# Moving the modulation products and the scores in a two-layer retention/mLSTM trunk

## The chip, the cores and the metric

The kernel runs on one core of a Trainium2 chip, as one program. The core has a matrix engine (TensorE, PE in the profile), three engines for elementwise work (VectorE or DVE, ScalarE or ACT, GpSimd or POOL) and SyncE (SP), which here only issues transfers from the chip's main memory. Each engine runs its own list of instructions in order; the engines wait for each other through semaphores, and a transfer is waited for in the same way. The metric is the device time of one execution in microseconds (us), as the median of several.

## The reference

The reference computes two decoder layers on 512 tokens of width 1024, in float32. In layer 0 the token mixer is retention with four heads, in layer 1 it is an mLSTM with four heads; each is followed by a gated convolutional feed-forward part. Before each of these four parts the state is normed and modulated by six vectors that come from the condition `c`:

```python
c_act = jax.nn.silu(c)
for i in range(DEPTH):
    mod = c_act @ ada_w[i] + ada_b[i]
    sh_t, sc_t, gt_t, sh_f, sc_f, gt_f = [m[:, None, :] for m in jnp.split(mod, 6, axis=-1)]
    h = rmsnorm(x, norm_tok_g[i]) * (1.0 + sc_t) + sh_t
    y = retention_mixer(h, ...) if i % N_MIXERS == 0 else mlstm_mixer(h, ...)
    x = x + gt_t * y
    h = rmsnorm(x, norm_ffn_g[i]) * (1.0 + sc_f) + sh_f
    x = x + gt_f * conv_ffn(h, ...)
return rmsnorm(x, final_g)
```

The product `c_act @ ada_w[i] + ada_b[i]` gives 6 x 1024 numbers for each layer. A head of a mixer needs its projections q, k, v and g (the gate); then scores between keys and queries with a decay (retention) or with exponential gates (mLSTM); the scores times v; a group norm over the head; the gate; and the product with `w_out`, which is added to the state.

## The kernel before, in words

**Layout and precision.** The state `x` and all activations lie transposed: 128 features on the partitions, the 512 tokens along the free dimension. Every float32 operand of a matrix product is kept as a high and a low half, so that one product is three matmuls (L281 to L283, `mm3`: high times high, low times high, high times low). An activation is split into `Pair`s (`split`: the high part on ScalarE, the low part on VectorE, L277 and L278). A weight tile is loaded into `raw` by SyncE (L182), its high part `whi` is made on ScalarE (L164) and its low part `wlo` on VectorE (L169).

**Items.** The program is first collected as a list of items (`item`). Most items are one weight tile's products: a tile of q, k or g (`proj_item`, 8 x 3 matmuls of 512 columns), a quarter of a head's v (`v_items`, which fills four PSUM banks and splits them after its fourth item, `vl`), or a tile of `w_out` with the residual add. Others have no weight and call a step of a head. At the end of the program the items are run through in order; `Ahead` issues the loads and the splits of coming weight tiles some items early. On each engine the framework's scheduler then sets the order of the instructions, from its own estimates, when the program is built; inside the folded part (below) the order is the written one. So the order on an engine need not be that of the list.

**Heads.** `heads` is used by both layers. It sets the order of the four heads' steps: q(i) (four items), v(i), the scores S(i), g(i), the attention A_(i), `mid_` (centring for the group norm), `end_` (the norm's root and the gate product y) and the output tiles o(i). For a head i of 1 or 2 the scores stand right behind v(i) and ahead of g(i). The scores (`ml_scores` in layer 1) load a row `mb` and a row `db` through SyncE, broadcast over the partitions, make the weights `w` from them, multiply the products `psc` by them (`sp`) and split the result (`sh`, `sl`) in four strips of 512, 384, 256 and 128 columns. In layer 0 the weights are a decay tile, `tab`. The attention (`pav`) takes these strips times v, and is followed in layer 1 by the denominator (`pden`). `mid_` sums the head (`zs`, whose low part is `zsl`; product `pmu`) and its squares (`zv`, added on GpSimd; low part `zvl`); `end_` multiplies these (`pvar`), takes a reciprocal root (`grs`) and makes the four tiles y.

**Modulations.** A modulation is one column of 128 of the 12,288 numbers: SyncE loads a 128 x 1025 block of `ada_w` (512.5 KB) into one of the two buffers of the pool `asides`, and VectorE multiplies it by `c_ext` and sums along the row (L140, `gemv`, through `side_work`). The first 16 are made at the start. The other 80 wait in the list `side`. The loop at the end of the program takes them off it, behind items that have weights and are `free`: ahead of the first folded part one for each such item, two for every tenth item, until LATER = 32 are left; behind it one for each item with an odd number. Eight of the 32 are taken inside the folded part of layer 0 itself (`modulate`): there the load is issued in every second unit, and the product follows `low_24` of a later unit. The scheduler is asked to keep these products in program order.

**Folded part.** Most of the feed-forward part of a layer runs in `folded`. It forms sums of weight halves first (`wa`, `wb`, `ws`, `wt`), so that fewer products are needed; the low parts of three of the sums are made by an accumulating transfer that GpSimd issues (L176). The weight chunks of the down product share the pool `asides`. In this case its units run from about 495 to 735 us in layer 0 and from about 1261 to 1506 us in layer 1. `bars` holds the item numbers of these two parts.

Of the kernel before, what the change touches and what calls it, by code (L numbers as in the profile page):

```python
# [15 lines left out]
P = 128  # L16
T = 512
D = 1024
KT = D // P
# [9 lines left out]
RAWS = 6  # L29
LATER = 32  # L30
FOLD_FROM = 5
# [4 lines left out]
SPLIT = 4  # L36
# [34 lines left out]
def trunk(ctx: ExitStack, tc: tile.TileContext, xT, cb, pos, vec, decay, zmask, ada, w_s0, w_in0, w_v0,  # L71
# [29 lines left out]
    def aside(s):  # L101
        return asides.tile([P, D + 1], F32, tag="a", name=uid(s))
# [306 lines left out]
    def folded(folds, h, terms, pairs, downs, modulate):  # L409

        no = lambda *a: None
        banks, sums, other = {}, {}, []

# [24 lines left out]
        def unit(i):  # L440
# [129 lines left out]
    def v_items(w_v, hd, h, v, split, between=lambda j: None):  # L570
# [18 lines left out]
        for j in range(4):  # L589
            item([Use(w_v[hd, j], 2 * T)], mk(j))  # L590
            between(j)
# [37 lines left out]
    def boundary(late, last, norm):  # L629


        for u, _ in late + last:
            u.off = OFF
        for p, after in ((0, lambda m: norm.square(0, m)), (1, norm.later)):
            for n, (u, run) in enumerate(late):
                item([u], lambda w, run=run, p=p, n=n: run(w[0], *HALVES[p], lead=p + n == 0), False)
                if p:
                    norm.beside()
            for u, run in last:
                item([u], lambda w, run=run, p=p, after=after: run(w[0], *HALVES[p], after), False)  # L640
        norm.rest()
# [37 lines left out]
    class Start(Norm):  # L679
# [24 lines left out]
        def rest(self):  # L704
# [4 lines left out]
            def products(w, p, k0, k1):  # L709
# [8 lines left out]
            item(uses, lambda w: products(w, 0, 0, SPLIT), False)  # L718
# [3 lines left out]
            item(uses, lambda w: products(w, 0, SPLIT, KT), False)  # L722
            item([], lambda w: self.use(1, 4, 8))
# [5 lines left out]
            if self.folded:  # L729
                item([], lambda w: self.sums())  # L730
            item(uses, end, False)

# [142 lines left out]

    def heads(st, q, v, s, g, a, mid, end, o, norm, at_last):

# [9 lines left out]
        v(1, at(1, mid_, 0))  # L887
        S(1)
        end_(0)
        g(1)  # L890
        A_(1)
# [3 lines left out]
        v(2, at(0, end_, 1))  # L895
        S(2)
        g(2)
        A_(2)
# [16 lines left out]
    class Ffn:  # L915
# [77 lines left out]
        def items(self, norm):  # L993
# [3 lines left out]
            downs = [p for gi in range(len(GROUPS) - 1) for p in self.down(gi)]  # L997
            steps, run = folded(folds, self.h, self.start.terms, pairs, downs, self.layer == 0)

# [235 lines left out]

    def ret_g(i):
        for j in range(4):
            proj_item(w_in0[i * 8 + 4 + j], h0, ret_gate(i))

    def ret_o(i):  # L1240
# [4 lines left out]
          ret_scores, ret_g, ret_attend, lambda i: None, ret_end, ret_o,  # L1245
          ffn0.start, RET_LAST)

# [118 lines left out]

    def ml_g(i):
        for j in range(4):
            proj_item(w_in1[1 + i * 8 + 4 + j], h1, ml_gate(i))

# [3 lines left out]
    def ml_v(i, between=nothing):  # L1374
# [6 lines left out]
    heads(M, ml_q, ml_v, ml_scores, ml_g, ml_attend, lambda i: gn_center(M[i]), ml_end, ml_o,  # L1381
          ffn1.start, ML_LAST)
    ffn1.items(End())
# [14 lines left out]
    for n, (uses, fn, free) in enumerate(items):  # L1398
        while ahead.at < len(ahead.flat) and ahead.may(n):
            ahead.load()  # L1400
            ahead.high()
            ahead.low()
        fn([u.chunk for u in uses])
        if not uses or not free or n <= 6:
            continue
        if n < bars[0]:
            for _ in range(2 if n > 20 and n % 10 == 0 else 1):
                if len(side) > LATER:
                    side_work(*side.pop(0))
        elif side and n % 2:  # L1410
            side_work(*side.pop(0))
    assert not side
# [104 lines left out]
```

## Time and profile before

| what | value |
|---|---|
| median of 3 runs | 1560.03 us (1559.39 to 1560.14) |
| the profiled execution | 1554.46 us |
| its span, from the first to the last instruction | 1552.7 us |
| mean granted TensorE clock | 0.992 |
| instructions | 23173 |
| VectorE, busy | 1200.5 us (77%) |
| ScalarE, busy | 861.2 us (55%) |
| GpSimd, busy | 229.3 us (15%) |

All times inside the kernel are from one profiled execution and are counted from its first instruction. A row of the profile names the source line, the engine, the operation, and output <- input by the names of the program, without buffer numbers; `wlo<-raw,whi` is the low part of a weight tile. In a timeline, a row begins with its start and its length, and what stands in brackets at its end is how long the engine was idle before it and what it waited for. SPq and POOLq are the queues on which SyncE and GpSimd issue transfers. A matmul's recorded end is modelled: successive matmuls overlap in the rows, and the distance between their starts tells their real pace. Short waits of TensorE can therefore show up as a longer distance between starts and not as idle time.

### The profile page before, as it was taken

What the parts mean: (1) busy time and instruction counts of PE and PEld (TensorE: products, weight loads), DVE (VectorE), ACT (ScalarE), POOL (GpSimd) and SP (SyncE); (2) the same over time, 40 slices, a digit from 0 to 9 for tenths busy, and PEclk for the clock granted to TensorE, in tenths of its full rate; (3) what the DMA queues carried; (4) which work ended last, traced back from release to release, by engine and by line L of the source; (5) the groups of instructions that cost most, each with busy time, mean ns of one, the idle gap of its engine ahead of it and who ended that gap; (6) DMA issues with size and microseconds to landing.
All of it is one profiled execution on the core that took longest, in us unless ns stands there. A gap on an engine that the chain in (4) does not pass through costs nothing. (4 is left out here: it accounts for less than half of the span.)

```text
span 1552.7 us, 23173 instructions
## 1 busy us (share of the span) xinstructions
PE 1513.2 (97%) x8996; PEld 1337.2 (86%) x8996; DVE 1200.5 (77%) x1814; ACT 861.2 (55%) x1282; POOL 229.3 (15%) x242
## 2 busy tenths in 40 slices
PE   7999999999999999999999999999999999999997
PEld 4788888888988999998988878888889889999997
DVE  8985768786997878887777777777588977787775
ACT  4534524443456767676655554554545666767763
POOL 3421001110130111111110011001022201111102
PEclk9999999999999999999999999999999999999999
DMA  8753464655315888887444433443312258777751
GB/s 312 228 186 109 143 188 159 204 177 167 110 42 136 210 208 205 230 195 202 160 128 149 149 109 105 152 144 112 126 54 72 67 135 198 195 191 188 187 140 55
DMA packets 72224, 241.79 MB, mean 156 GB/s; under 512 B 9761, under 2 KB 12065, under 8 KB 72114
## 3 DMA queue, kind: packets, MB, share of 16 engines
q1 hardware_dynamic: 59730, 195.22, 38.4%
q0 software_dynamic: 12384, 45.09, 15.3%
q8 instruction: 70, 1.15, 0.3%
q14 instruction: 40, 0.33, 0.1%
HBM read 193.06 MB, written 2.12 MB: 126 GB/s over the span
## 5 line engine op out<-in xcount | busy, mean ns | idle before, releaser
L164 ACT CAST whi<-raw 128x1024 fp32r<-128x1024 f32 (+1 forms) x190 | 194.3, 1029 | 144.4 <-PE pp L282 58.3
L169 DVE TENSOR_TENSOR wlo<-raw,whi 128x1024 fp32r<-128x1024 f32 (+1 forms) x158 | 191.5, 1219 | 46.7 <-ACT whi L164 46.1
L281 PE MATMUL pp<-hh,whi 128*128 128x512 f32 x560 | 218.4, 390 | 2.3 <-DVE vl L278 2.0
L282 PE MATMUL pp<-hl,whi 128*128 128x512 f32 x560 | 218.1, 390 | 0.0
L283 PE MATMUL pp<-hh,wlo 128*128 128x512 f32 x560 | 218.0, 389 | 0.0
L595 DVE SCALAR_TENSOR_TENSOR x<-po,mod,x 128x512 f32<-128x512 f32 (+1 forms) x184 | 114.2, 629 | 71.6 <-PE po L283 68.0
L282 PE MATMUL po<-ggl,whi 128*128 128x512 f32 (+1 forms) x448 | 154.0, 345 | 0.0
L283 PE MATMUL po<-ggh,wlo 128*128 128x512 f32 (+1 forms) x448 | 153.5, 344 | 0.0
L281 PE MATMUL po<-ggh,whi 128*128 128x512 f32 (+1 forms) x448 | 153.0, 345 | 0.0
L422 PE MATMUL p<-hh,whi 128*128 128x256 f32 x544 | 150.6, 277 | 0.0
L423 PE MATMUL p<-hl,whi 128*128 128x256 f32 x544 | 150.4, 276 | 0.0
L424 PE MATMUL p<-hh,wlo 128*128 128x256 f32 x544 | 150.4, 276 | 0.0
L140 DVE SCALAR_TENSOR_TENSOR ada<-ada,c_ext 128x1025 f32<-128x1025 f32 x93 | 115.7, 1245 | 32.3 <-DMA ada<-ada 32.2
L281 PEld LDWEIGHTS pp<-hh,whi 128*128 128x128 f32 x560 | 105.2, 188 | 24.6 <-DVE vl L278 2.5
L283 PEld LDWEIGHTS pp<-hh,wlo 128*128 128x128 f32 x560 | 105.2, 188 | 21.8
L282 PEld LDWEIGHTS pp<-hl,whi 128*128 128x128 f32 x560 | 105.2, 188 | 21.4
L281 PE MATMUL po<-yh,whi 128*128 128x256 f32 (+1 forms) x352 | 115.8, 329 | 0.0
L282 PE MATMUL po<-yl,whi 128*128 128x256 f32 (+1 forms) x352 | 115.6, 328 | 0.0
L283 PE MATMUL po<-yh,wlo 128*128 128x256 f32 (+1 forms) x352 | 115.6, 328 | 0.0
L927 ACT ACTIVATE cv<-p,vecs 128x512 f32<-128x512 f32 x68 | 53.1, 780 | 96.2 <-PE p L424 57.3
L932 DVE SCALAR_TENSOR_TENSOR cv<-p,vecs,cv 128x511 f32<-128x511 f32 (+1 forms) x136 | 101.0, 745 | 2.2
L422 PEld LDWEIGHTS p<-hh,whi 128*128 128x128 f32 x544 | 102.2, 188 | 0.1
(287 smaller groups left out, 3986.9 us busy)
## 6 DMA issues: line engine op xcount, KB each, us to landing
ada<-ada SPq DMA_DIRECT2D x96, 512.5 KB, 4.0
raw<-w_in SPq DMA_DIRECT2D x62, 512.0 KB, 3.8
wb<-w_up SPq DMA_DIRECT2D x34, 512.0 KB, 4.4
wa<-w_up SPq DMA_DIRECT2D x34, 512.0 KB, 5.3
wlo<-wa POOLq DMA_DIRECT2D x34, 512.0 KB, 4.6
wlo<-ws POOLq DMA_DIRECT2D x34, 512.0 KB, 4.9
raw<-w_o SPq DMA_DIRECT2D x32, 512.0 KB, 3.5
raw<-w_dn SPq DMA_DIRECT2D x32, 512.0 KB, 4.4
```

The source lines that it names most:

```text
L140: return V.scalar_tensor_tensor(raw, raw, 1.0, c_ext[:], op0=ALU.mult, op1=ALU.mult, accum_out=mods[layer][:, f : f + 1])
L164: A.copy(hi, w[:, r])
L169: V.tensor_tensor(lo, w[:, r], hi.bitcast(F32), op=ALU.subtract)
L281: PE.matmul(o, ah, bh, start=start, stop=False)
L282: PE.matmul(o, ah, bl, start=False, stop=False)
L283: PE.matmul(o, al, bh, start=False, stop=stop)
L422: PE.matmul(o, hi[:, ch], b[0], start=st, stop=False, skip_group_check=True)
L423: PE.matmul(o, hi[:, ch], b[1], start=False, stop=False, skip_group_check=True)
L424: PE.matmul(o, lo[:, cl], b[0], start=False, stop=sp, skip_group_check=True)
L595: V.scalar_tensor_tensor(x[m][:, r], ps[:, r], gate_col, x[m][:, r], op0=ALU.mult, op1=ALU.add)
L927: A.activation(acc[:], ps[:], AF.Identity, bias=col("fcb", self.layer * 2 * FT + f), scale=self.conv_col(f, 2))
L932: V.scalar_tensor_tensor(acc[:, s:], ps[:, : T - s], self.conv_col(f, j), acc[:, s:], op0=ALU.mult, op1=ALU.add)
```

## The change

The eight modulations inside the first folded part are gone, with the code for them. `free` is now a number of modulations for an item, or a pair of numbers: one for an item ahead of the first folded part, and one for an item behind it. Ahead of it (LATER = 24 are left) a v item of heads 1 to 3 and a gate item of layer 0 take 1, 2, 1, 2 for their four items, and any other free item takes 1. Behind it only v items of heads 1 to 3 and gate items of layer 1 take one each; q, k and output items take none, nor does anything of head 0. In layer 1 (`s_at` = 0) the scores of heads 1 and 2 move from right behind v(i) to right behind the first gate item of the same head; in layer 0 (`s_at` = -1) they stay. So in layer 1 `end_(0)` now follows v(1) directly.

```diff
-LATER = 32
+LATER = 24
...
-    def item(uses, fn, free=True):
+    def item(uses, fn, free=1):
...
-        items.append((uses, fn, free))
+        items.append((uses, fn, free if isinstance(free, tuple) else (free, 0)))
...
-    def proj_item(src, h, then):
+    def proj_item(src, h, then, free=1):
...
-        item([Use(src, KT * P)], fn)
+        item([Use(src, KT * P)], fn, free)
...
                 f.high_24()
                 f.low_24(i % 2)
-                if other:
-                    layer, m, after, raw = other.pop()
-                    gemv(layer, m, raw)
-                    after()
...
             load_down(i + 2)
-            if modulate and side and i % 2 == 0 and i + 2 < len(folds):
-                layer, m, after = side.pop(0)
-                raw = aside("ada")[:]
-                nc.sync.dma_start(raw, ada[layer, m])
-                other.append((layer, m, after, raw))
...
-            item([Use(w_v[hd, j], 2 * T)], mk(j))
+            item([Use(w_v[hd, j], 2 * T)], mk(j), (1 + (hd > 0 and j % 2), hd > 0))
...
         q(1, at(1, S, 0))
         A_(0)
         v(1, at(1, mid_, 0))
-        S(1)
+        if s_at < 0:
+            S(1)
         end_(0)
-        g(1)
+        g(1, at(s_at, S, 1))
         A_(1)
         contract_items(o(0))
         mid_(1)
         q(2)
         v(2, at(0, end_, 1))
-        S(2)
-        g(2)
+        if s_at < 0:
+            S(2)
+        g(2, at(s_at, S, 2))
         A_(2)
...
-    def ret_g(i):
+    def ret_g(i, between=nothing):
         for j in range(4):
-            proj_item(w_in0[i * 8 + 4 + j], h0, ret_gate(i))
+            proj_item(w_in0[i * 8 + 4 + j], h0, ret_gate(i), 1 + j % 2)
+            between(j)
...
-    def ml_g(i):
+    def ml_g(i, between=nothing):
         for j in range(4):
-            proj_item(w_in1[1 + i * 8 + 4 + j], h1, ml_gate(i))
+            proj_item(w_in1[1 + i * 8 + 4 + j], h1, ml_gate(i), (0, 1))
+            between(j)
...
         fn([u.chunk for u in uses])
-        if not uses or not free or n <= 6:
-            continue
-        if n < bars[0]:
-            for _ in range(2 if n > 20 and n % 10 == 0 else 1):
-                if len(side) > LATER:
-                    side_work(*side.pop(0))
-        elif side and n % 2:
-            side_work(*side.pop(0))
+        late = n > bars[0]
+        for _ in range(free[late] if uses and n > 6 else 0):
+            if len(side) > (0 if late else LATER):
+                side_work(*side.pop(0))
```

The remaining lines of the diff only pass 0 in place of `False` and drop the argument `modulate`.

More of the change, by code (lines that the diff above doesn't have):

```diff
@@ L406, in fn, with folded @@
             then(ps)
-        item([Use(src, KT * P)], fn)
-    def folded(folds, h, terms, pairs, downs, modulate):
+        item([Use(src, KT * P)], fn, free)
+    def folded(folds, h, terms, pairs, downs):
         no = lambda *a: None
-        banks, sums, other = {}, {}, []
+        banks, sums = {}, {}
         def product(i, n, o, start=False):
@@ L639, in boundary @@
             for u, run in last:
-                item([u], lambda w, run=run, p=p, after=after: run(w[0], *HALVES[p], after), False)
+                item([u], lambda w, run=run, p=p, after=after: run(w[0], *HALVES[p], after), 0)
         norm.rest()
@@ L717, in products @@
                             k == 0, k == KT - 1)
-            item(uses, lambda w: products(w, 0, 0, SPLIT), False)
+            item(uses, lambda w: products(w, 0, 0, SPLIT), 0)
             item([], lambda w: self.root(1))
@@ L730, in rest @@
                 item([], lambda w: self.sums())
-            item(uses, end, False)
+            item(uses, end, 0)
         def sums(self):
@@ L874, in gn_root, with heads @@
         st["rs"] = rs
-    def heads(st, q, v, s, g, a, mid, end, o, norm, at_last):
+    def heads(st, q, v, s, g, a, mid, end, o, norm, at_last, s_at):
         def on(fn, i):
@@ L997, in items @@
             downs = [p for gi in range(len(GROUPS) - 1) for p in self.down(gi)]
-            steps, run = folded(folds, self.h, self.start.terms, pairs, downs, self.layer == 0)
+            steps, run = folded(folds, self.h, self.start.terms, pairs, downs)
             def early(n):
```

8 lines of the change are left out of this document (4 added, 4 removed).

## The prediction

> **What bounds the kernel now.** I read the page first (busy shares, groups, issues), then the busy time of chosen stretches, then TensorE's waits, then the timeline around each of them.
>
> ```profile
> span 1552.7 us, 23173 instructions
> PE 1513.2 (97%) x8996; PEld 1337.2 (86%) x8996; DVE 1200.5 (77%) x1814; ACT 861.2 (55%) x1282; POOL 229.3 (15%) x242
> L140 DVE SCALAR_TENSOR_TENSOR ada<-ada,c_ext 128x1025 f32<-128x1025 f32 x93 | 115.7, 1245 | 32.3 <-DMA ada<-ada 32.2
> ada<-ada SPq DMA_DIRECT2D x96, 512.5 KB, 4.0
> ```
>
> TensorE is busy for 97% of the span. A modulation (L140) costs VectorE 1.24 us and its 512 KB load lands 4.0 us after issue; VectorE already waits 32 us for such loads. The change leaves TensorE's work as it is, so it can only move TensorE's idle time. Busy time by stretch (columns: window, PE, PEld, DVE, ACT, POOL, clock, DMA share, GB/s):
>
> ```profile
> 495.00:735.00 240.00, 239.77 (x1720) 223.65 (x1719) 192.07 (x307) 170.01 (x233) 34.40 (x40) 1.00 0.82 205
> 880.00:920.00 40.00, 37.69 (x180) 30.55 (x179) 32.56 (x49) 19.52 (x31) 9.51 (x9) 1.00 0.40 129
> ```
>
> TensorE's waits (what it waited for; total, times, longest):
>
> ```profile
> PE p L424 <- DMA wlo<-wt: 2.1, 1, 2.1
> PE pp L281 <- DVE vl L278: 2.0, 1, 2.0
> PE pvar L291 <- DVE vl L278: 1.3, 1, 1.3
> PE pav L282 <- DVE sl L278: 0.6, 2, 0.4
> PE pden L291 <- ACT o L1328: 0.5, 1, 0.5
> PE pmu L292 <- DVE zsl L278: 0.3, 1, 0.3
> ```
>
> The first folded part, from which the modulations go, has TensorE full (239.77 of 240). The idle that the change can reach is the 2.1 us behind the fold (wlo<-wt), the 2.31 us of the stretch with the second block's first attention and root, the 2.0 us before its third head's gate (pp), and the 0.5 us at pden.
>
> **The change, part by part.** Places in the changed kernel come from the order of each engine's instructions in the built programs; GpSimd's order is the same in both. Terms are against the profiled execution.
>
> *First fold.* Eight modulations of 1.24 us leave VectorE: 0 by themselves, since TensorE is full there. Their loads go too. The last collides with a weight load just behind the fold:
>
> ```profile
> 727.47 0.33 SPq L139 DMA_DIRECT2D ada<-ada  x1
> 727.18 0.86 POOL L176 DMA_DIRECT2D wlo<-wt  x1 [1.90 <-ACT wlo L175]
> wlo<-wt POOLq DMA_DIRECT2D x1, 512.0 KB, 10.2
> 737.38 0.38 PE L424 MATMUL p<-t24h,wlo 128*128 128x256 f32 x1 [2.07 <-DMA wlo<-wt]
> ...
> wlo<-wt POOLq DMA_DIRECT2D x1, 512.0 KB, 6.4
> ```
>
> The last row is the same load in the second fold, which has no modulation: 6.4 us against 10.2, and no wait. In the changed order the two modulation loads that run ahead stand before the last weight chunks, not beside this one. Landing 3.8 us sooner covers the 2.07. I take **-2.1**; ends 0 (the weights alone fill the engines) and -2.1.
>
> *Second block, attention of head 0.* Four modulations stood ahead of or among its score splits; none does now.
>
> ```profile
> 877.16 1.23 DVE L140 SCALAR_TENSOR_TENSOR ada<-ada,c_ext 128x1025 f32<-128x1025 f32 x1 [2.33 <-DMA ada<-ada]
> 879.73 0.39 PE L281 MATMUL pav<-sh,vh 128*128 128x512 f32 x1
> 889.31 0.40 PE L291 MATMUL pden<-sumsh,ones 128*128 128x512 f32 x1
> 940.59 0.39 PE L281 MATMUL pav<-sh,vh 128*128 128x512 f32 x1
> 946.37 0.39 PE L281 MATMUL pav<-sh,vh 128*128 128x512 f32 x1
> ```
>
> Head 1's attention (last two rows: three of four groups in 5.78 us, so 7.71 for all) has no wait; head 0's takes 9.58. The difference is 1.87, more than the waits' 0.67 because short waits hide inside modelled matmul ends. The one at 877.16 cost 1.23 and its wait 2.33, a second stands among the splits: over twice that. **-1.9**, ends -1.9 and -1.0. The mean sum behind it (pmu) gets its split sooner: **-0.4**, ends -0.6 and 0.
>
> *Root of head 0.* It followed head 1's scores and still waited 1.3 us. Now it stands right behind the last value tile, without those scores (912.78 to 918.12 less the wait: 4.0 us) to cover it.
>
> ```profile
> 912.78 0.39 PE L281 MATMUL psc<-mqkh,mqkh 128*128 128x512 f32 x1
> 918.12 0.50 PE L291 MATMUL pvar<-zvh,ones_v 128*128 128x512 f32 x1 [1.33 <-DVE vl L278]
> 910.82 2.07 DVE L140 SCALAR_TENSOR_TENSOR ada<-ada,c_ext 128x1025 f32<-128x1025 f32 x1
> 911.77 2.28 POOL L841 TENSOR_TENSOR zv<-zq,zq 128x512 f32<-128x512 f32 x1
> ```
>
> But the modulation at 910.82 now comes behind the split that it waits for, and its PSUM bank is no longer the value tiles'. The split would be ready at 911.4 to 912.4 and TensorE there at about 910.4: a wait of 1 to 2. **-0.2**, ends -0.8 and +0.7.
>
> The modulation at 910.82 took 2.07 us beside a GpSimd add, against 1.22 to 1.24 elsewhere. The Trainium skill ("SBUF — State Buffer", Who interferes with whom) says that VectorE with two SBUF inputs and a GpSimd instruction that reads SBUF exclude each other on a shared port. The trace agrees (0.84 us more). By that rule each modulation leaving the fold, where GpSimd only issues loads, for a stretch with GpSimd adds may cost about 0.85 more of VectorE, an estimate from these rows; if one of them met a late split the sum would rise by that, to about -0.3.
>
> *Attention of head 1: the new wait.* Scores of head 1 move three tiles nearer to it. Their mask row (mb) is loaded through SyncE's queue, in order.
>
> ```profile
> 917.31 5.69 DMA mb<-scratch
> ...
> mb<-scratch SPq DMA_DIRECT2D x2, 256.0 KB, 4.3
> ...
> 923.03 0.35 DVE L1314 SCALAR_TENSOR_TENSOR w<-mb,bcols,zm 128x128 f32<-128x128 f32 x1 [3.05 <-DMA mb<-scratch]
> 927.30 0.68 DVE L278 TENSOR_TENSOR sl<-sp,sh 128x512 fp32r<-128x512 f32 x1
> 936.95 0.68 DVE L872 TENSOR_TENSOR grs<-pvar,den 128x512 f32<-128x512 f32 x1
> 949.26 1.22 DVE L140 SCALAR_TENSOR_TENSOR ada<-ada,c_ext 128x1025 f32<-128x1025 f32 x1
> ...
> ada<-ada SPq DMA_DIRECT2D x1, 512.5 KB, 5.8
> ```
>
> Before, it was issued at 917.31, and the first split (sl) was ready at 927.98, over 12 us ahead of the attention at 940.59. In the changed order six modulation loads stand ahead of mb on SyncE. Only two modulation buffers exist, so a load waits for the modulation two before its own, and the last of the six waits for the last modulation ahead of the scores on VectorE. That one stands behind head 0's root and norm: the run from grs to the last y took 949.26 - 936.95 = 12.3 us, here with three more modulations (3.7 us) in it, from about 917 (an estimate: root's split at 912, the four value splits that take 2.48, two modulations). So it ends about 932.6 and mb is issued at 933.1. It lands 4.3 (the stretch's row of issues) to 5.69 us later: 937.4 to 938.8. From landing to first split before: 927.98 - 923.02 = 4.96 us, of which 0.6 was a weight split in between: 4.4. So the split is ready at 941.8 to 943.2. TensorE arrives at 940.59 less the 2.5 won since 879: 938.1. Wait +3.7 to +5.1; I take **+4.4**, the middle. Low end +1.5 (loads chained tighter by 2.5 us), high end +8 (two chained loads at 5.8, as beside the fold's weights in the last row, instead of 4.0). What goes with it: the wait for pden behind this attention, **-0.5**.
>
> The Trainium skill ("DMA: Bandwidth & Descriptors", Anatomy of one DMA) gives a load 2.0 us plus its bytes at 436 GB/s, measured on GpSimd's path; 256 KB would land in 2.6 us, an estimate by that page. The trace does not agree: 4.3 and 5.69 for this load on SyncE's queue. By the page's figure the wait would be some 2.0 and the sum about -3.1.
>
> *Head 2.* Its first gate product waited the 2.0 us (pp) for a bank that the value splits held; those stood behind head 1's root and norm on VectorE, until 1021.
>
> ```profile
> 949.93 0.23 PE po L282
> ...
> 1021.00 2.48 DVE L278 TENSOR_TENSOR vl<-pv,vh 128x512 fp32r<-128x512 f32 x4
> ```
>
> With the scores behind the first gate tile, that tile takes the bank that the scores took, and its 24 products of 512 columns (5.5 us at 0.23, a step of the chain) cover the splits: **-2.1** (the first product's 0.50 instead of 0.39 goes too), ends -2.1 and 0. Its attention then meets splits about in time: 0 to +1, taken as 0.
>
> *Last attentions.* In the second block five modulations now precede head 3's splits: **+0.4**, ends 0 and +1.2 (one modulation). In the first block eight more modulations (9.9 us) must fit; most are hidden. At head 3's attention seven of them, instead of two, stand between the value splits and the last score split:
>
> ```profile
> 358.39 0.69 DVE L1094 TENSOR_TENSOR sp<-psc,tab 128x512 f32<-128x512 f32 x1 [3.75 <-DMA tab<-decay]
> 361.68 0.39 PE L281 MATMUL pav<-sh,vh 128*128 128x512 f32 x1
> 364.76 0.40 PE L281 MATMUL pav<-sh,vh 128*128 128x512 f32 x1
> 364.01 0.29 DVE L278 TENSOR_TENSOR sl<-sp,sh 128x128 fp32r<-128x128 f32 x1 [0.36 <-ACT sh L277]
> ```
>
> Three of them stand among the splits, and each waits for a load that can issue only when the modulation two before it is done: one per 4 us or so. The first moves little, since the decay tile (tab) was late before too. The last moves from 364.3 to about 369.2 (the sixth modulation ends by 359, then two loads of 4.0, with their modulations, follow one another). TensorE can work on the other strips until about 367, so its wait grows from 1.15 (the first group takes 364.76 - 361.68 = 3.08, against the 1.93 of a group above) to about 2.9: **+1.7**, ends 0 and +4. Two more table loads on ScalarE (55% busy) cost nothing unless at a late split.
>
> Sum: -2.1 - 1.9 - 0.4 - 0.2 + 4.4 - 0.5 - 2.1 + 0.4 + 1.7 = **-0.7**. The profiled execution took 1554.46 us and the median of three runs 1560.03, 5.6 above it; carried over, 1559.3.
>
> **The rivals.** *Faster:* the loads chain faster, so that head 1's wait is 1.5 and the first block's is 0: -0.7 - 2.9 - 1.7 = -5.3, 1554.7. For it: every gain is a wait in the trace. Against it: the queue's order.
> *Slower:* SyncE's queue. Each modulation load waits for a buffer and the mask behind it: +8 at head 1 and +4 in the first block give -0.7 + 3.6 + 2.3 = +5.2, 1565.2. It decides where the mask lands later than about 942.
> *The fold's wait stays* (weight loads alone fill the engines): +1.4, 1561.4. It is still no measurable change.
>
> **How the numbers follow.** About 0.2% (3.1 us) is what a measurement can tell. Small net change, with or without the fold's wait: 0.42, 1557 to 1563 being its own range. Faster rival: 0.33. Slower: 0.25. The range from 1553 to 1565 takes in both other cases and leaves out the ends where all gains or all losses meet.
>
> **What would show it.** Right: TensorE's waits for wlo<-wt, for vl at the third head and for sl in head 0's attention are gone, and one of 4 to 5 us for sl stands at head 1's attention, with mb issued near 933. Wrong: mb is issued by 925, or attention of head 3 in the first block waits over 5 us.

## The result, and the profile after

The changed kernel takes 1568.92 us (median of four runs, 1567.79 to 1570.44), the kernel before 1559.71 beside it (1557.86 to 1560.14): a ratio of 1.0058, with a 95% interval of 1.0043 to 1.0073. It is slower by 9.2 us. 1559.3 was forecast, with a range that ended at 1565.

The profiled execution of the changed kernel took 1568.66 us, close to its median. The page of the changed kernel, as in the prediction's first fence:

```profile
span 1566.9 us, 23173 instructions
...
PE 1519.5 (97%) x8996; PEld 1338.9 (85%) x8996; DVE 1204.0 (77%) x1814; ACT 863.6 (55%) x1284; POOL 228.9 (15%) x242
...
L140 DVE SCALAR_TENSOR_TENSOR ada<-ada,c_ext 128x1025 f32<-128x1025 f32 x93 | 117.7, 1271 | 42.4 <-DMA ada<-ada 42.3
```

The work is the same. VectorE waits 42 us for modulation loads instead of 32 (38 in a second profile of the kernel before): modulations that came out of the fold stand closer together, and 23 instead of 18 waits are for a load. Their mean time also rose, 1245 to 1271 ns. TensorE's waits of the changed kernel (what it waited for; total, times, longest), attention rows and those of the root:

```profile
PE pav L281 <- ACT sh L277: 8.5, 6, 3.6
...
PE pav L282 <- DVE sl L278: 3.7, 4, 1.7
...
PE pvar L291 <- ACT zvh L277: 1.5, 1, 1.5
```

The rows of the fold (wlo<-wt) and of the third head's gate (pp for vl) are gone, as forecast. In their place the attention products (pav) wait 12.2 us, in ten waits, for score splits (sh, sl). In the first profile of the kernel before, such waits came to 0.9 us (0.6 for sl, 0.3 for sh), in the second, taken later, to 2.7.

The listed waits are not the whole loss, because short waits hide inside the modelled ends of matmuls. So I added up, by place, the distance between the starts of successive matmuls beyond 0.227 us for 512 columns, and in proportion for fewer (own sum from the traces, us, good to some tenths). The second profile of the kernel before stands beside the first:

| place (window) | before, 1st | before, 2nd | changed |
|---|---|---|---|
| first block, head 0's attention (120-160) | 1.1 | 1.1 | 5.7 |
| first block, head 3's attention (360-400) | 1.4 | 6.6 | 8.4 |
| end of the fold to the second block (720-840) | 8.4 | 8.1 | 5.8 |
| second block, attentions of heads 0 and 1, root (880-960) | 5.6 | 5.4 | 11.3 |
| second block, head 2's gate (1000-1040) | 2.3 | 3.8 | 0.0 |
| second block, head 3's attention (1120-1160) | 1.0 | 1.0 | 3.5 |
| whole kernel | 61.0 | 68.2 | 75.2 |

Against the second profile of before, 7.0 us more are lost: +4.6 and +1.8 in the first block, -2.3 at the fold, +5.9, -3.8 and +2.5 in the second block, and -1.7 left over in other places. Two places of the first block and two of the second lose; the fold and the third head's gate gain. The profiled executions lie 14.2 and 7.1 us apart, where the medians lie 9.2 apart: the first profile of before is faster than its median and the second (1561.54) slower.

**Head 1 of the second block.** Timeline rows of the changed kernel (start, length, engine, line, tile; in brackets the wait and its end):

```profile
936.29 7.15 SPq L139 DMA_DIRECT2D ada<-ada  x3
943.54 0.37 SPq L1302 DMA_DIRECT2D mb<-scratch  x1
...
950.05 0.35 DVE L1309 SCALAR_TENSOR_TENSOR w<-mb,bcols,zm 128x128 f32<-128x128 f32 x1 [3.91 <-DMA mb<-scratch]
...
952.97 0.69 DVE L278 TENSOR_TENSOR sl<-sp,sh 128x512 fp32r<-128x512 f32 x1
...
959.99 0.39 DVE L278 TENSOR_TENSOR sl<-sp,sh 128x128 fp32r<-128x128 f32 x1 [0.36 <-ACT sh L277]
...
948.35 0.39 PE L283 MATMUL pp<-hh,wlo 128*128 128x512 f32 x1
...
952.37 1.22 PE L281 MATMUL pav<-sh,vh 128*128 128x512 f32 x2 [3.63 <-ACT sh L277]
...
962.97 0.40 PE L291 MATMUL pden<-sumsh,ones 128*128 128x512 f32 x1
```

The mask row (mb) stands behind the modulation loads on SyncE's queue; the last three of them take 7.15 us to issue, since they wait for buffers, and it is issued at 943.54. VectorE then waits 3.91 us for it, and TensorE 3.63. But the loss doesn't end with the first strip: the last split of the four strips starts at 959.99, seven us after the first, and pden follows 10.6 us after the attention's start (962.97 - 952.37), where the kernel before needed 8.35 (7.7 of products and 0.65 for pden). From the last gate product to pden it is 14.62 us; before it was 8.58.

**Head 0 of the second block.** No modulation stands ahead of its score splits or among them any more. Rows of the changed kernel:

```profile
886.86 0.69 DVE L278 TENSOR_TENSOR sl<-sp,sh 128x512 fp32r<-128x512 f32 x1 [0.69 <-ACT sh L277]
...
895.59 0.39 DVE L278 TENSOR_TENSOR sl<-sp,sh 128x128 fp32r<-128x128 f32 x1 [0.36 <-ACT sh L277]
...
887.74 0.84 PE L281 MATMUL pav<-sh,vh 128*128 128x512 f32 x3
...
897.26 0.40 PE L291 MATMUL pden<-sumsh,ones 128*128 128x512 f32 x1
```

From the first product to pden it still takes 9.52 us (897.26 - 887.74); before it was 9.58 (889.31 - 879.73). Each strip passes between VectorE and ScalarE several times, with a weight split in between, and the last split starts 8.7 us after the first. So the four strips set this pace without any modulation. Head 2's attention in the same execution shows the other side: three modulations stand among its splits, one of them after a wait of 0.86 us for its load, but its first split was ready 12 us ahead of TensorE, and it took 7.71 us without a wait. What counts is how far ahead the first split is.

**Head 0 of the first block.** The prediction did not look there. Timeline of the changed kernel:

```profile
120.73 0.55 DVE L1088 TENSOR_TENSOR sp<-psc,tab 128x384 f32<-128x384 f32 x1
123.33 1.23 DVE L140 SCALAR_TENSOR_TENSOR ada<-ada,c_ext 128x1025 f32<-128x1025 f32 x1 [2.05 <-DMA ada<-ada]
124.48 0.55 DVE L278 TENSOR_TENSOR sl<-sp,sh 128x384 fp32r<-128x384 f32 x1
...
125.09 0.44 PE L282 MATMUL pav<-sl,vh 128*128 128x384 f32 x1 [1.68 <-DVE sl L278]
```

A modulation that belongs to a value tile of the next head has been placed between the product (sp) and the split (sl) of one strip of head 0's scores. VectorE waits 2.05 us for its load, multiplies for 1.23, and only then makes the split that TensorE waits for. Behind these waits the clock is down as well (columns: window, PE, PEld, DVE, ACT, POOL, clock, DMA share, GB/s):

```profile
128.00:131.00 3.00, 3.00 (x11) 2.72 (x12) 2.06 (x4) 0.94 (x2) 2.39 (x2) 0.56 0.42 156
```

TensorE is busy throughout with data that are there, but starts only 11 matmuls.

**Head 3 of the first block.** Stretches of the changed kernel (the same columns), then rows of its timeline:

```profile
370.00:374.00 4.00, 2.50 (x7) 1.82 (x7) 4.00 (x9) 1.59 (x3) 0.00 (x0) 0.59 0.49 160
374.00:378.00 4.00, 4.00 (x17) 3.67 (x16) 3.60 (x8) 0.47 (x2) 0.00 (x0) 0.56 0.66 194
378.00:382.00 4.00, 4.00 (x28) 3.83 (x27) 2.28 (x4) 1.78 (x4) 0.00 (x0) 1.00 0.89 297
```

```profile
364.54 1.23 DVE L140 SCALAR_TENSOR_TENSOR ada<-ada,c_ext 128x1025 f32<-128x1025 f32 x1 [2.80 <-DMA ada<-ada]
...
376.47 0.29 DVE L278 TENSOR_TENSOR sl<-sp,sh 128x128 fp32r<-128x128 f32 x1
...
368.72 0.51 PE L281 MATMUL pav<-sh,vh 128*128 128x512 f32 x1 [2.88 <-ACT sh L277]
```

A modulation again, a load again (2.80), a late split; and behind the waits the granted clock is 0.56 to 0.59 until about 378. With VectorE busy for all of 370 to 374, it is VectorE's list that sets the pace.

### The profile page after: what moved, and what is told of

It reads as the page before. It is cut to its first block, busy times and chain, and to the rows that moved or that the text cites. A ratio compares the mean times of both kernels' runs of the same rounds, so it can differ in the third digit from the quotient of the medians.

```text
span 1566.9 us, 23173 instructions
## 1 busy us (share of the span) xinstructions
PE 1519.5 (97%) x8996; PEld 1338.9 (85%) x8996; DVE 1204.0 (77%) x1814; ACT 863.6 (55%) x1284; POOL 228.9 (15%) x242
## 4 chain that ended last, share of the span: by engine, by line
PE 79%; DVE 13%; issue 3%; ACT 2%; DMA 2%; POOL 1%; SPq 0%; DVEq 0%; ACTq 0%; POOLq 0%
PE po L281 7%; PE po L282 7%; PE po L283 7%; PE pp L281 7%; PE p L423 7%; PE pp L282 7%; PE pp L283 7%; PE p L425 7%; PE p L424 7%; PE pv L574 3%; PE pv L575 3%; PE pv L576 3%; DVE wlo L169 2%; DVE ada L140 2%; DVE hl L343 1%
## 5 line engine op out<-in xcount | busy, mean ns | idle before, releaser
L140 DVE SCALAR_TENSOR_TENSOR ada<-ada,c_ext 128x1025 f32<-128x1025 f32 x93 | 117.7, 1271 | 42.4 <-DMA ada<-ada 42.3
```

The costliest lines, as they stand in the source:

```text
L140: return V.scalar_tensor_tensor(raw, raw, 1.0, c_ext[:], op0=ALU.mult, op1=ALU.mult, accum_out=mods[layer][:, f : f + 1])
```

## The experiments

The theory after this reading: late splits come from *a serial list on VectorE*, in which each modulation costs its load too, because only two buffers exist. Rivals: SyncE's queue (the mask behind the loads) is all of it; the moved scores are the cause, whatever the modulations do; or TensorE's lower clock is the cost, not the waits. All ratios are against the kernel before, run beside each.

**Scores back behind the value tiles.** In the changed kernel:

```diff
-          ffn1.start, ML_LAST, 0)
+          ffn1.start, ML_LAST, -1)
```

> The changed kernel with the scores of heads 1 and 2 of the second block put back behind the value tiles; modulations as changed. Theory (the loss sits where modulations and their loads stand ahead of a head's score splits): the mask of head 1 is again issued ahead of the root, so the 3.63 us wait at head 1's attention and the slow clock behind it go (7.8 us of lost time there to under 1), and the wait of about 2 us at head 2's first gate product comes back; about 5.5 us under the changed kernel, near 1563.5. Rival 1 (eight more modulations ahead of the fold overload VectorE): no change, about 1569. Rival 2 (the move of the scores is the whole loss): 1559 or below.

Measured 1569.14 us, ratio 1.0061 [1.0038, 1.0084]: as slow as the change itself. Nothing of the expected 5.5 us was won, and the wait moved. Rows of this kernel:

```profile
950.64 3.35 DVE L296 RECIPROCAL grs<-grs 128x512 f32<-128x512 f32 x1 [2.04 <-ACT grs L295]
...
960.20 2.07 ACT L1323 ACTIVATE o<-pp 128x512 f32<-128x512 f32 x4
...
960.85 0.80 PE L291 MATMUL pden<-sumsh,ones 128*128 128x512 f32 x1 [5.65 <-ACT o L1323]
```

Now the scores come early, with modulations among their splits, and head 0's root and norm come late behind them; the gate's sigmoid (o) stands behind the norm on ScalarE, and TensorE waits 5.65 us at pden for the bank. Scores, root, norm and modulations are one list on VectorE: whichever stands last is waited for. That the scores' move alone is the cause is out.

**First block and fold alone.** The changed kernel, with the second block as before (the line above, and):

```diff
-        for _ in range(free[late] if uses and n > 6 else 0):
+        k = (free != (0, 0) and n % 2) if late else free[0]
+        for _ in range(k if uses and n > 6 else 0):
```

> The first block and the fold as changed (56 modulations ahead of the fold, none in it), the second block as before (modulations behind every odd item, scores behind the value tiles). Theory: the first block's two losses (4.6 us at head 0's attention, 7.0 at head 3's) stay, the fold's gain of 2.6 too: about 8 to 9 us slower than before in profiled time, 1564 to 1568. Rival 2 (scores): no slower than before, 1557 to 1560.

Measured 1561.96, ratio 1.0015 [1.0004, 1.0026], less than the 1564 to 1568 expected. By place: 3.5 us are lost at head 0 of the first block and 7.6 at head 3, where the kernel before lost 1.1 and 6.6 in its second profile. So only head 0's loss stands out, and the fold's gain of some 2 us stands against it.

**Second block alone.** The changed kernel with LATER = 32 and with the fold's eight modulations and the first block's old rule put back.

> The second block as changed, the first block and the fold as before (48 modulations ahead, 8 in the fold). Theory: +7.8 at head 1's attention, +2.5 at head 3's, -2.0 at head 0's, -2.3 at head 2's gate: about 6 us slower than before, 1563 to 1566. Rival 1 (VectorE's load ahead of the fold): no slower than before, at or under 1560.

Measured 1565.26, ratio 1.0037 [1.0025, 1.0049], as expected. Heads 0 and 1 lose 9.9 us here, and head 0 of the first block only 1.4 (the profiled execution, 1561.82, was the fastest of ten). The two halves cost 2.2 and 5.5 us over the 1559.73 of the kernel before beside them; together 7.8 of the 9.2. The larger part is the second block's rule.

**The fold's eight modulations into the first block's old free items.** In the kernel before, LATER = 24, and:

```diff
-            if modulate and side and i % 2 == 0 and i + 2 < len(folds):
+            if False and modulate and side and i % 2 == 0 and i + 2 < len(folds):
```

> The kernel before with the fold's eight modulations moved ahead of it by the old rule (24 left instead of 32); nothing else. By the built order the eight then stand in the first feed-forward part's items, behind the last attention. Theory (where a modulation stands decides): the 2.1 us wait behind the fold goes and nothing comes: about 2 us faster than before, 1557 to 1558. Rival 1 (56 modulations ahead of the fold are too many for VectorE): several us slower than before, 1563 and more.

Measured 1562.96, ratio 1.0022 [1.0011, 1.0033]. A gain was expected. The wait for wlo at the fold's end did go, but at the fold's start this row of TensorE's waits is new:

```profile
PE p L423 <- DVE hl L278: 2.9, 1, 2.9
```

The loss at 480 to 520 rises from 0.7 to 7.2 us. In the changed kernel that place loses 0.2, so this belongs to the old rule with eight more modulations ahead of the fold, not to the change. Why the fold's first split comes late there was not followed further.

**The mask's queue.** The changed kernel, with the three small loads of each head issued from GpSimd, away from the modulation loads:

```diff
-        nc.sync.dma_start(tab[:], decay[i])
+        nc.gpsimd.dma_start(tab[:], decay[i])
...
-        nc.sync.dma_start(mb[:], scratch[i : i + 1].broadcast_to([P, T]))
-        nc.sync.dma_start(db[:], scratch[4 + i : 5 + i].broadcast_to([P, T]))
+        nc.gpsimd.dma_start(mb[:], scratch[i : i + 1].broadcast_to([P, T]))
+        nc.gpsimd.dma_start(db[:], scratch[4 + i : 5 + i].broadcast_to([P, T]))
```

> The changed kernel with the loads of the decay tile (tab) and of the mask rows (mb, db) issued by GpSimd instead of SyncE; the order on VectorE stays. Queue theory (the mask stands behind modulation loads on SyncE): the 3.91 us that VectorE waits for mb at head 1 go, and with them most of the 3.63 us wait at head 1's attention and its half-clock stretch: 4 to 5 us under the changed kernel, 1564 to 1565. Chain theory (what is late is VectorE's list of root, norm and six modulations, in whatever order): at most 1 us, 1568 to 1569.

Measured 1568.40, ratio 1.0056 [1.0041, 1.0071]. The queue theory said 1564 to 1565. Rows of this kernel at head 1:

```profile
946.57 0.35 DVE L1309 SCALAR_TENSOR_TENSOR w<-mb,bcols,zm 128x128 f32<-128x128 f32 x1
...
950.59 0.73 PE L281 MATMUL pav<-sh,vh 128*128 128x512 f32 x2 [1.43 <-ACT sh L277]
```

VectorE no longer waits for the mask, and starts the score's first step 3.5 us earlier (946.57 against 950.05). TensorE's first wait falls from 3.63 to 1.43. But the rest is still paced by the splits: 12.13 us from the last gate product to pden (948.77 to 960.90) instead of 14.62. The queue is 2.5 of the 6 us lost there, and the whole kernel didn't gain. In this execution head 3 of the first block lost 10.4 (8.4 in the changed kernel) and head 3 of the second 1.5 more; why was not followed.

**The scores' move alone.** The kernel before, with only the scores of heads 1 and 2 of the second block moved behind the first gate tile.

> The kernel before with only the move of the scores (heads 1 and 2 of the second block, behind the first gate tile); modulations as before. Chain theory: without the extra modulations head 0's root and head 1's scores both fit ahead of head 1's attention, head 2's gate no longer waits 2 us for a bank: 1 to 2 us under the kernel before, 1557.5 to 1559. Rival (scores so close to the attention cost by themselves): 4 us or more above it.

Measured 1562.09, ratio 1.0014 [1.0003, 1.0024]; a small gain was expected. The gain at head 2 came (0.0 us lost there), the cost at heads 0 and 1 as well (10.4 against 5.4):

```profile
922.74 0.50 PE L291 MATMUL pvar<-zvh,ones_v 128*128 128x512 f32 x1 [2.96 <-ACT zvh L277]
...
953.37 0.50 PE L281 MATMUL pav<-sh,vh 128*128 128x512 f32 x1 [1.28 <-DVE sp L1321]
```

The root has lost its cover (2.96), and the scores come just too late with the old number of modulations: from the last gate product to pden it takes 10.45 us instead of 8.58.

**Head 1 of the second block free of modulations.** The changed kernel, with the eight of head 1's value and gate items moved to head 0's output and head 2's q items:

```diff
-            item([Use(w_v[hd, j], 2 * T)], mk(j), (1 + (hd > 0 and j % 2), hd > 0))
+            item([Use(w_v[hd, j], 2 * T)], mk(j), (1 + (hd > 0 and j % 2), hd > 1))
...
-        contract_items(o(0))
+        contract_items(o(0), free=(1, 1))
...
-            proj_item(w_in1[1 + i * 8 + 4 + j], h1, ml_gate(i), (0, 1))
+            proj_item(w_in1[1 + i * 8 + 4 + j], h1, ml_gate(i), (0, i > 1))
```

> The changed kernel with the eight modulations of head 1's value and gate tiles in the second block put behind the output tiles of head 0 and the q and k tiles of head 2. Chain theory: nothing but root and norm stand ahead of head 1's scores, so its attention does not wait and the clock stays up: 6 to 8 us under the changed kernel, 1561 to 1563. Queue theory without the chain: the same mask load, nothing ahead of it, so also 4 to 5 us. If neither: 1569.

Measured 1563.89, ratio 1.0033 [1.002, 1.0047], 5.0 us less than the changed kernel (6 to 8 were expected). No wait is left at head 1's attention, and its mask is issued 11 us earlier (943.54 in the changed kernel):

```profile
932.28 0.38 SPq L1302 DMA_DIRECT2D mb<-scratch  x1
...
947.70 0.39 PE L283 MATMUL pp<-hh,wlo 128*128 128x512 f32 x1
...
956.46 0.40 PE L291 MATMUL pden<-sumsh,ones 128*128 128x512 f32 x1
```

That is 8.76 us from gate to pden, as before the change (8.58). Here the modulations were moved and nothing else, the scores staying where the change put them, and the 6 us were gone: the modulations ahead of the scores are shown as the cause at head 1. This run takes them off VectorE's list and their loads out of SyncE's queue at once. The run with the mask on GpSimd's queue tells the two apart: 2.5 us are the queue, the rest is the list. Of the gain 3.3 us are lost again at head 2, where modulations now stand among its score splits.

**TensorE kept busy.** Behind those waits the granted clock is down, so a rival says that the clock, not the wait, is what costs. The changed kernel with 16 extra matmuls ahead of two attentions (head 3 of the first block, head 1 of the second), into a bank that the attention then overwrites:

```diff
+            for n in range(fill if vt == 0 else 0):
+                PE.matmul(ps[:], ones["1"][:], v[0].hi[:], start=True, stop=True)
...
-        attend(st["s"], st["v"], evac)
+        attend(st["s"], st["v"], evac, 16 * (i == 3))
...
-        attend(st["s"], st["v"], evac)
+        attend(st["s"], st["v"], evac, 16 * (i == 1))
```

> The changed kernel with 16 more matmuls of 512 columns ahead of two attentions (head 3 of the first block, head 1 of the second), written into a PSUM bank that the attention then overwrites; they take the place of TensorE's waits there (16 x 0.227 = 3.6 us against waits of 2.88 and 3.63 us). Clock theory (a wait of 3 us and more halves the granted clock for about 4 us behind it): the half-clock stretches behind both waits go, 2 us each: about 4 us under the changed kernel, 1565. Rival (only the waits count): no change or slightly slower, 1569.

Measured 1573.61, ratio 1.0083 [1.0066, 1.01]: worse. At head 1 of the second block, the stretch behind the wait in the changed kernel, and then the one behind the extra matmuls, where the attention starts at 958.03:

```profile
955.00:958.00 3.00, 3.00 (x10) 2.51 (x10) 1.72 (x4) 1.42 (x4) 1.38 (x2) 0.53 0.27 108
```

```profile
958.00:961.00 3.00, 2.35 (x8) 1.35 (x9) 2.15 (x4) 1.15 (x4) 0.33 (x1) 1.00 0.44 123
```

The clock stayed at 1.00, and yet gate to pden took 14.21 us (953.80 to 968.01) against 14.62. The half clock there costs next to nothing, since splits arrive slower than even the slow TensorE uses them. That the kernel became slower by 4.7 us is mostly from the other place, and is taken up under the hardware.

**The kernel before, once more.** Unchanged, one profile.

> The kernel before once more, for a second profiled execution. The one shown took 1554.46 us, 5 us under the median, and the kernels that keep its first block (e3, e4, e6) lose 4.2 to 7.0 us at head 3's attention of the first block, where it lost 1.4. If the first profile was a lucky one there: 4 us or more at that place now, and a time near 1560. If not: 1.4 us again.

Measured 1561.54 us, span 1559.8. At head 3's attention in the first block:

```profile
356.69 0.38 SPq L1091 DMA_DIRECT2D tab<-decay  x1
...
362.95 0.69 DVE L1094 TENSOR_TENSOR sp<-psc,tab 128x512 f32<-128x512 f32 x1 [5.58 <-DMA tab<-decay]
...
364.41 0.50 PE L281 MATMUL pav<-sh,vh 128*128 128x512 f32 x1 [1.83 <-ACT sh L277]
```

The decay tile's wait is 5.58 us here and was 3.75 in the profile of the prediction. The place loses 6.6 us instead of 1.4, and the executions above that keep the old first block (second block alone, the fold's modulations moved, scores alone) lost 4.2 to 7.0. The first profile was a lucky execution at this place. Of the 7.1 us between the two profiles 5.2 lie here.

**The queue, in the kernel before.** The same three lines as above, put into the kernel before.

> The kernel before with the loads of the decay tile and the mask rows issued by GpSimd instead of SyncE, nothing else. Queue theory: VectorE waits 3.75 us (5.3 to 5.8 in e3, e4, e6) for the decay tile at head 3 of the first block because the load is issued late on SyncE; issued by GpSimd it comes earlier and 2 to 4 us go: 1556 to 1558. Rival (the load is as late on GpSimd's list, or the weights' loads take its place): 1559 to 1561.

Measured 1557.34, ratio 0.9984 [0.9974, 0.9993], 2.8 us less, as expected. Head 3 of the first block loses 0.2 us; the profiled execution was the slowest of eleven all the same (1560.55), with about 2 us more lost at the fold's end than in the second profile of before, and as much at heads 0 and 1 of the second block. The decay tile's loads, in the second profile of before and then in this kernel, where the last of the four issues is head 3's:

```profile
DMA to landing us min/median/max: 5.2/5.7/6.2
```

```profile
L1091 POOL DMA_DIRECT2D tab<-decay x4: 592/600/788, 116.3 to 351.5; - x4
...
DMA to landing us min/median/max: 3.1/3.3/4.4
```

**Head 1's value items with one modulation each in the first block.** In the changed kernel:

```diff
-            item([Use(w_v[hd, j], 2 * T)], mk(j), (1 + (hd > 0 and j % 2), hd > 0))
+            item([Use(w_v[hd, j], 2 * T)], mk(j), (1 + (hd > 1 and j % 2), hd > 0))
```

> The changed kernel with one modulation, not two, behind the second and fourth value tiles of head 1 in the first block; the two left over go to later tiles ahead of the fold, so their number there stays 56. By the built order no modulation stands among the score splits of head 0 in the first block any more. Theory: the 2.05 us wait for its load, its 1.23 us and the half-clock stretch go, 4.6 us at that attention: 3 to 5 us under the changed kernel, 1564 to 1566. Rival (another wait takes its place at the next head, or the loss there is chance): 1568 to 1569.

Measured 1565.57, ratio 1.0033 [1.0021, 1.0046]: 3.4 us less than the changed kernel, as expected. Stretches of the changed kernel and of this one:

```profile
100.00:160.00 60.00, 57.29 (x265) 48.01 (x264) 35.73 (x52) 23.27 (x39) 11.10 (x13) 0.97 0.37 119
```

```profile
100.00:160.00 60.00, 59.78 (x290) 50.83 (x290) 37.78 (x53) 24.41 (x41) 12.32 (x17) 1.00 0.36 118
```

TensorE is full again and the lost time at head 0's attention falls from 5.7 to 1.0 us. The second modulation of head 1's value items was the one among head 0's splits. Nor was the loss there chance: in the other runs with the changed first block this place lost 3.5 to 6.9 us, in those with the old one 0.6 to 1.4.

**A version from these findings.** The kernel before, with the three loads on GpSimd's queue; the fold keeping its modulations except the last (the one beside wlo); no modulation in the second block before head 1's value tiles; only head 2's scores behind the first gate tile; and what that displaces put at the output items of heads 0 and 1 and at head 3's q items. The core of it:

```diff
-            if modulate and side and i % 2 == 0 and i + 2 < len(folds):
+            if modulate and side and i % 2 == 0 and i + 4 < len(folds):
...
+        marks.append(len(items))
...
-        contract_items(o(0))
+        contract_items(o(0), free=2)
...
-        S(2)
-        g(2)
+        if s_at < 0:
+            S(2)
+        g(2, at(s_at, S, 2))
...
-        elif side and n % 2:
+        elif side and n >= marks[1] and (n % 2 or free == 2):
```

> The kernel before with what gained in the changed one and without what lost: the last of the fold's eight modulations moved behind the fold (wait of 2.1 us), none at head 0 of the second block (1.9), only head 2's scores behind its first gate tile (2.2), the extra modulations at head 0's output tiles and later, and the decay and mask loads on GpSimd. Chain theory: 5 to 7 us under the kernel before, 1553 to 1555. If the places where modulations are added lose again as much as is won: 1559 to 1561.

Measured **1549.26 us**, ratio 0.9936 [0.9922, 0.995]: 10.8 us less than the kernel before and 19.7 less than the changed one, and 4 us better than expected. Of this kernel's page, and of its waits all that remain at the places of the change:

```profile
span 1547.2 us, 23164 instructions
...
PE 1511.6 (98%) x8996; PEld 1335.1 (86%) x8996; DVE 1198.7 (77%) x1814; ACT 862.3 (56%) x1283; POOL 233.4 (15%) x254
```

```profile
PE pden L291 <- ACT o L1331: 0.9, 1, 0.9
...
PE pav L281 <- DVE sp L1321: 0.6, 1, 0.6
PE pvar L291 <- DVE vl L278: 0.5, 1, 0.5
```

The lost time is 55.4 us against 68.2: 0.2 at head 3 of the first block (6.6), 5.8 around the end of the fold (8.1), 0.1 at head 2's gate (3.8). Head 0's attention of the second block, for which 1.9 us were counted, took 9.52 us here too. The queue alone gave 2.8 us; the other parts of this version were not run apart.

## Why the prediction was wrong

The net change was put at -0.7 us and came out at +9.2. By its steps, each against the first profile, which it used, and where that differs against the second:

- *First fold, -2.1:* right. The wait for wlo is gone and the load lands in 7.4 us; -2.6 measured.
- *Second block, attention of head 0, -1.9:* this step failed. The attention took 9.52 us against 9.58. The prediction put its whole distance to head 1's 7.7 us down to the modulations at its splits. With them gone the four strips came at the same pace. The listed wait for sl did go, as the prediction's sign said, but one of 0.6 for sp came in its place.
- *Mean sum and root, -0.4 and -0.2:* about -0.1 and +0.1 (own sums from the starts), inside their bounds.
- *Head 1's attention and pden (+4.4 and -0.5, together +3.9):* measured +6.0 (14.62 - 8.58). The mechanism was right, with its first wait (3.63 measured, 3.7 to 5.1 forecast): the loads chained through two buffers, the mask issued 21.2 us after the root's mean (943.54 - 922.30; on the prediction's clock it is 933.1 less 912). Mis-sized is the term of +4.4. It took the first strip's split for the whole wait. The other three strips followed at VectorE's and ScalarE's pace, and the products took 10.6 us instead of 7.7, for 2.9 us more. The last split was 7 us behind the first, and the prediction had no row for that. These three steps come to +5.9 in place of +1.4; the table's rows give 5.7.
- *Head 2, -2.1:* right, -2.3 measured, and by itself too with only the scores moved.
- *Head 3 of the second block, +0.4:* mis-sized; +2.5. Ahead of its first split stands a modulation that waited 2.6 us for its load. No run undid this.
- *First block, "most are hidden":* this step failed too, by omission. +4.6 us at head 0's attention had no term. The order of the built program put a modulation of the next head's value tile among head 0's splits, and the prediction looked at that order only for head 3. The single-modulation run takes it back (5.7 to 1.0).
- *Head 3 of the first block, +1.7:* +7.0 against the first profile and +1.8 against the second. The number agrees with the second, but for part of a wrong reason: the row used as the base (tab's wait of 3.75) was that of a lucky execution. So the agreement is luck.
- *Carrying over to the median.* The prediction added 5.6 us to the profile's time, as if the gap lay somewhere untouched. The second profile says otherwise: 5.2 of the 7.1 us between the two lay at head 3 of the first block, one of the places it costed.

The slower rival (1565.2, 0.25) had the right sign and named SyncE's queue. The runs give it a part only: 2.5 us at head 1 with the queue moved, and nothing in the whole kernel. What decides at head 1 is the list on VectorE: with the queue moved 12.13 of the 14.62 us were left, with the modulations moved 8.76. The side estimate for modulations beside GpSimd adds wrongly: 0.85 more on -0.7 is about +0.15 and not -0.3. Nothing else rests on it.

Still open: head 3 of the first block, where the changed kernel loses 1.8 us more than the second profile of before and no run took that back; what the other parts of the fastest version give one by one, why the old rule with more modulations is late at the fold's start, and the 2.5 us at head 3 of the second block.

## What to carry to other kernels

A helper operation with its own load and two buffers costs its load's time, not its 1.2 us, when it is placed closely after others; read where the built order puts it among the critical splits of every head, not only where the diff mentions one. Cost a late chain by its last strip, not by its first, and before putting a long stretch down to one operation, look for a like stretch without that operation. And take a second profile of the base before using one wait of it as a term, and give small urgent loads a queue in which no large load waits for a buffer ahead of them.

## What the hardware showed

**Half clock after short waits.** In the run with extra matmuls the first block's attention of head 3 had short waits behind them, and then ran at 0.50 for some 10 us. Its rows and stretches:

```profile
371.77 0.44 PE L282 MATMUL pav<-sl,vh 128*128 128x384 f32 x1 [1.29 <-DVE sl L278]
...
373.81 0.58 PE L281 MATMUL pav<-sh,vh 128*128 128x256 f32 x1 [1.40 <-ACT sh L277]
```

```profile
370.00:373.00 3.00, 1.07 (x3) 0.48 (x3) 3.00 (x8) 0.94 (x1) 0.00 (x0) 0.88 0.33 85
373.00:376.00 3.00, 1.73 (x4) 1.08 (x4) 2.58 (x5) 0.70 (x2) 0.00 (x0) 0.50 0.79 258
378.00:382.00 4.00, 4.00 (x15) 3.61 (x14) 1.88 (x4) 0.59 (x1) 0.00 (x0) 0.50 0.94 298
```

The mean of 0.88 in 370 to 373 puts the drop near 372.25, so a wait of 0.27 and the one of 1.29 us came before it, and the one of 1.40 falls into the slow stretch. In 378 to 382 TensorE had its data and was busy throughout, at 0.50; the changed kernel was back at 1.00 there. From the last product before this attention to the first one behind it this kernel took 20.4 us (364.96 to 385.33) and the changed one 16.1 (365.46 to 381.58). So the half clock cost where data were ready, and next to nothing at head 1, where they weren't. Behind the last wait it cost this kernel some 2.8 us (an estimate: the products took 8.8 us, 376.51 to 385.33, and at the usual pace they take 6.0). But the 4.3 us between the two kernels are not the clock's alone. The changed kernel has a slow stretch there too, and the order differs: with the extra matmuls TensorE ran all strips of the first output tile before the second, and waited for the late ones, where the changed kernel went on with other tiles. The changed kernel shows the same at head 0 of the first block: 0.56 in 128 to 131, behind waits of 1.68, 0.21 and 0.59 us. In the run that takes these waits away the clock there stays at 1.00. No run varied the length of a wait by itself. The Trainium skill ("TensorE: Matmul & The Clock Gate", Part 1: The HAM clock gate) says that the clock goes to one half after an idle window of about 3.4 us that runs freely. The trace agrees in the size of the drop; but here 0.27 and 1.29 us of waiting came before it, with matmuls between, so less than a full window of idling was enough. In the clock records of these two kernels the slow stretches last 3.4, 6.8, 6.8 and 10.2 us, one to three times 3.4.

**A small load on another queue.** The decay tile landed 3.3 us after issue from GpSimd's queue and 5.7 from SyncE's. At head 3 it was also issued 5.2 us earlier (351.5 against 356.69, where SyncE had issued a modulation load just ahead of it, at 356.27). The Trainium skill ("DMA: Bandwidth & Descriptors", Issuing engines are not separate DMA queues) says that DMAs from all issuers run on the same DMA engines and interleave there. No run here measures bandwidth by queue. What the three moved loads won is an earlier issue and a quicker landing, together 2.8 us of the kernel before.
